# Product-key layer: batched second one-hot scaled on ScalarE, half the gate moves on VectorE, more products ahead of the run

## The chip, the cores and the metric

The kernel runs on one core of a Trainium2 chip, as one launch. The metric is the device time of an execution in microseconds. Five engines work side by side and each takes its own instructions in order: TensorE (PE; its weight loads are PEld), VectorE (DVE), ScalarE (ACT), GpSimd (POOL) and SyncE (SP), which here only issues transfers. They wait for one another by semaphores.

## The reference, cut to what matters

Two transformer blocks with mixtures of experts run first, then a block with a convolution and a recurrence. The change touches what stands at the very end, a product-key expert layer over 512 tokens of 1024 features. For each token and each of 8 heads it picks 16 of 128 x 128 experts and a gate for each; every expert is a row of `peer_u` and a row of `peer_v`.

```python
s1 = jnp.einsum('bshd,hnd->bshn', q[..., :half], peer_k1)
s2 = jnp.einsum('bshd,hnd->bshn', q[..., half:], peer_k2)
v1, i1 = lax.top_k(s1, PEER_TOPK)
v2, i2 = lax.top_k(s2, PEER_TOPK)
cand = (v1[..., :, None] + v2[..., None, :]).reshape(bsz, seq, PEER_HEADS, PEER_TOPK * PEER_TOPK)
sc, ci = lax.top_k(cand, PEER_TOPK)
experts = (jnp.take_along_axis(i1, ci // PEER_TOPK, axis=-1) * PEER_NKEYS
           + jnp.take_along_axis(i2, ci % PEER_TOPK, axis=-1))
gates = jax.nn.softmax(sc, axis=-1)
...
u_sel = jnp.take(peer_u, eb, axis=0)
z = jnp.einsum('td,tkd->tk', hb, u_sel)
act = jax.nn.gelu(z, approximate=False) * gb
return jnp.einsum('tk,tkd->td', act, jnp.take(peer_v, eb, axis=0))
```

## The kernel before

Tokens 384 to 511 (the last of four tiles) are done by rows: each of their 128 picks gathers a row of `peer_u` and a row of `peer_v` for 128 tokens at once (`row`, on GpSimd's queue), VectorE takes the dot product (`dot`) and adds the row times its gelu and gate (`add`). Tokens 0 to 383 are done densely: all 128 blocks of 128 experts are multiplied out, and a table `gd` of gates, zero where an expert was not picked, is multiplied onto the result.

A dense block a has two halves. `zed(a)` is the product of a block of `peer_ut` with the tokens: 8 steps of 3 matmuls (24 of 384 columns), then a gelu on ScalarE. The result stays in one of NZ = 17 tiles or, for the last ND blocks, goes to DRAM (`zd`) and comes back. The y half multiplies the result with the gates (`hid`, on GpSimd) and takes 18 matmuls of 512 columns with a block of `peer_v`. Each weight is split in two parts (`weight`): ScalarE rounds it to `whi`, and another engine subtracts to get `wlo`; the matmuls with `wlo` wait for that. Raw, high and low parts have four buffers each.

The layer runs in this order. `peer_pre` normalizes. `peer_pick` takes the picks (`peer_top`, then a loop over the tiles 3, 0, 1, 2 on VectorE, with transposes on TensorE). `peer_gates` builds `gd`: for each 8 tokens, VectorE makes one-hots (`hots`: 128 places against rows, and against columns times the gate), TensorE multiplies them token by token in two groups of four, the results move out of PSUM into `stage`, and each 16 tokens are stored. After the last store, the run goes over the 128 blocks: a product `zed(a + NZ)` and the y half of block a, until no products are left, then y halves alone; `turns` spreads the gathered rows over them, FAST of them while there are products.

Products of the first blocks and of the last ND come ahead of the run. They are a generator, `more`, and `ahead(n)` takes n of its steps; `peer_pick` calls it once a tile and `peer_gates` twice in 8 tokens, and what is left is done after the gates. The order on each engine is not that of the code: a scheduler places the instructions by its own estimate, and `issue_after` adds a few constraints. Line numbers are those of the profile of before.

Of the kernel before, what the change touches and what calls it, by code (L numbers as in the profile page):

```python
# [18 lines left out]
NEG = -1.0e30  # L19
# [6 lines left out]
class Net:  # L26
    def __init__(self, nc, tc, ctx, A, out, dbg=None):
# [3 lines left out]
        # what the weights' splits are queued behind: those of the next chunks, and of all others  # L31
# [18 lines left out]
    def consts(self):  # L50
# [5 lines left out]
        # NEG where key > query, for the block on the diagonal  # L56
# [8 lines left out]
        # before[s, t] = 1 where s < t  # L65
# [3 lines left out]
        # 16, 15, ... 1  # L69
# [6 lines left out]
        # token and, less 2 ** 20, its rows among the results of first and second choices  # L76
# [5 lines left out]
        # tri[s, t] = 1 where s <= t  # L82
# [6 lines left out]
    def wtile(self, tag, dt):  # L89
        """The stream's own buffers and, where a layer has room for them, more"""  # L90
        if self.over:
            return self.over.tile([128, 1024], dt, tag=tag + "o", bufs=1, name=tag)
        k = self.turn[tag] = self.turn.get(tag, 0) + 1
        n = self.extra.get(tag, 0) if self.more else 0
        if n and k % (n + 4) >= 4:
            return self.more.tile([128, 1024], dt, tag=tag + "x", bufs=n, name=tag)
        return self.wp.tile([128, 1024], dt, tag=tag, bufs=4, name=tag)

    def raw(self, src, key=None):
        """key: of a chunk that may have been loaded ahead"""  # L100
# [7 lines left out]
    def weight(self, src, w=1024, eng=None, key=None):  # L108
        """One chunk of up to [128, 1024] as the sum of two float32r tiles."""
# [11 lines left out]
    def mm3(self, out, l, r, start, stop):  # L121
        """out += (l0 + l1)^T (r0 + r1) without the product of the two low parts."""
# [8 lines left out]
    def rsqrt(self, x, n, name, bufs=2):  # L131
        """1 / sqrt(x) of an SBUF tile [p, n], by a first guess and three Newton steps."""
# [15 lines left out]
    def silu_row(self, src, pool):  # L148
        """silu of a row of features, on all partitions"""
# [6 lines left out]
    def ada(self, c, w, mod, cols, how="V", bufs=3, lag=2):  # L156
        """The six vectors as columns: column 8 v + k of mod has the features 128 k .. of vector v; how: by turns on
        VectorE (V) or on GpSimd and ScalarE (S). A generator that stops after each column, so that other work can run
        between; a column is done lag steps later. Its weights come into bufs tiles of the pool self.ring."""
# [34 lines left out]
    def bcast_cols(self, out, cols, n=4):  # L194
        """out[m, 128 i + t] = cols[t, i]"""
# [5 lines left out]
    def col_sum(self, x, n, pool, square, acc=None):  # L201
        """Sums over the features of x [128, n, tokens] (squared) as columns [128 tokens, tiles] in PSUM; acc: the sums
        over n"""
# [32 lines left out]
    def spread(self, t, sh, hi, lo, c):  # L236
        """hi + lo = t + sh, which, where c is odd, also goes to t"""
# [9 lines left out]
    def rms(self, x, pool, acc=None):  # L247
        """1 / sqrt(mean square + eps) of the tokens of x [128, 8, tokens], tokens on partitions"""
# [6 lines left out]
    def modulate(self, x, r, a, sh, h, pool, bufs=3):  # L255
        """h = x * r * a + sh: whole, or split in two"""
# [17 lines left out]
    def first_mod(self, x, gain, c, w, mod, hp, pool):  # L274
        """h = rmsnorm(x) * gain * (1 + sc) + sh, features on partitions, split in two, while sh and sc come in"""
# [29 lines left out]
    def head(self, prep, o, pt, pool):  # L305
        """One head in stages; prep gives score(i, ps, n), which fills ps[:, :n] with the logits of query block i, and
        the values; o: [64 rows, 512] f32"""
# [47 lines left out]
    def heads(self, quart, oT, pool, steps, early, first):  # L355
        """quart(q), a generator, prepares four heads and leaves their prep functions in the list it is given. The
        stages of a head run between those of its neighbours; first, a generator, between those of the first four, and
        steps of each quarter's heads the conditioning's. early: steps of the second four before the first head."""
        nc = self.nc
        ready, run = [], []  # L360
        # the weights of query block i and key block j, keys on partitions, at i + 3 j
# [33 lines left out]
    def fox_cum(self, h, cq, ck, room, keep):  # L395
        """Running sums of the log forget gates, as bfloat16 parts: head 4 j + m on rows 32 m .. of cell j"""
# [44 lines left out]
    def fox_heads(self, h, oT, keep, pool):  # L441
# [7 lines left out]
        def quart(quart, ready):  # L449
            qk = []  # L450
            for which, g in ((0, gq), (1, gk)):
# [14 lines left out]
                # the query's rows also carry the softmax scale 1/8  # L466
# [14 lines left out]
        def prep(quart, hh, qk, v):  # L481
            st = []
            for which in range(2):
                raw, r = qk[which]
                # twice, for the high and the low part
# [31 lines left out]
    def proj_tok(self, ps, h, ws, i):  # L517
        """ps[tok, n] = h[:, tokens of tile i]^T w for a weight of n columns in chunks of 1024 / n K tiles"""
# [9 lines left out]
    def split(self, src, pool, tag):  # L528
        """[128, n, 512] float32 as the sum of two float32r tiles"""
# [9 lines left out]
    def out_proj(self, x, oT, w, g1, pool, then=None):  # L539
        """x += g1 * (o w), features on partitions; then(c), when x's chunk c is done"""  # L540
# [15 lines left out]
    def rope_tables(self, keep, pool):  # L556
        """cos and sin of position * frequency, [128 tokens, 4, 16]"""
# [12 lines left out]
        for name, quarter in (("cos", 0.25), ("sin", 0.0)):  # L570
            # turns, rounded to whole ones, then angle - turns * 2 pi in three parts of 2 pi
# [16 lines left out]
    def rope(self, eng, x, cs, n, pool):  # L588
        """Turns x[128, 4, n, 32] in place"""
# [27 lines left out]
    def mla_begin(self, stack, x, gain, mod):  # L617
        """The latent rows are r (a x)^T w + sh^T w for h = a x r + sh, with r to come: opens the pool of a x and w, on the
        side that the layer before has left already, and gives a generator that loads w and works out sh^T w, and what is
        to be done when x's chunk c is there"""  # L620
# [25 lines left out]
    def mla(self, x, cs, room, pool):  # L646
# [3 lines left out]
        # the latent rows of the tokens, normed, features on partitions  # L650
# [1646 lines left out]
```

## Time and profile before

| | |
|---|---|
| median of three runs | 3077.49 us (3072.53 to 3083.78) |
| span of the profiled execution | 3077.5 us |
| TensorE busy over the span | 2764.6 us, 90% |
| VectorE busy | 2363.3 us, 77% |
| ScalarE busy | 1314.5 us, 43% |
| GpSimd busy | 1334.4 us, 43% |
| HBM read and written | 562.59 MB and 61.01 MB |

The profiled execution's span is as long as the median run, so nothing has to be added for what lies around it. The shares are means over stages that differ: the product-key layer takes the span from about 1700 us on. In it `peer_top` ends near 1842, the loop over the picks near 1941, the gates near 2157, and the run near 3045; the rest is the last normalization. Each stage is to be read by itself, by the busy time of every engine in that stretch.

### The profile page before, as it was taken

To read this page: it belongs to the slowest core of one execution; us is meant where nothing else is said; L and a number is where in the kernel's file an instruction comes from. 1 tells how busy PE (TensorE), PEld (TensorE's weight loads), DVE (VectorE), ACT (ScalarE), POOL (GpSimd) and SP (SyncE) were. 2 spreads that over 40 slices of the span, in tenths; PEclk is the share of its full clock that TensorE was granted. 3 is DMA by queue.
4 is the path that set the end of the run, shared out by engine and by line. 5 is a ranking of instruction groups with operands and counts; after the bars stand their busy time and mean duration, and the time that the engine had idled before them with its cause. 6 is when DMAs were issued, how large, how long until landed. Compare 5 with 4: busy or idle time off the path is not lost.

```text
span 3077.5 us, 42494 instructions
## 1 busy us (share of the span) xinstructions
PE 2764.6 (90%) x14989; PEld 2247.0 (73%) x14989; DVE 2363.3 (77%) x4756; ACT 1314.5 (43%) x2352; POOL 1334.4 (43%) x926
## 2 busy tenths in 40 slices
PE   2999978997889798899889897899999999999996
PEld 2877556686545566666766687889899999999885
DVE  7998458758975686688974799999677777777777
ACT  3344437734564573532432533334333333333332
POOL 3111027633211573006850345433566666666553
PEclk9999879998899899999988998999999999999998
DMA  6775159924535795220021223565999999999893
GB/s 220 239 242 182 65 193 314 342 96 139 185 124 188 236 331 205 90 72 19 1 78 37 88 85 122 201 227 185 322 312 321 313 318 325 326 314 315 285 328 112
DMA packets 230881, 622.81 MB, mean 202 GB/s; under 512 B 32796, under 2 KB 92492, under 8 KB 227192
## 3 DMA queue, kind: packets, MB, share of 16 engines
q1 hardware_dynamic: 130960, 429.82, 41.3%
q0 software_dynamic: 45120, 154.42, 14.7%
q10 hardware_dynamic: 54568, 35.66, 4.0%
q8 instruction: 122, 2.00, 0.3%
q14 instruction: 111, 0.91, 0.1%
HBM read 562.59 MB, written 61.01 MB: 203 GB/s over the span
## 4 chain that ended last, share of the span: by engine, by line
PE 39%; DVE 20%; DMA 4%; issue 2%; ACT 1%; POOL 1%; POOLq 0%; ACTq 0%; DVEq 0%; SPq 0%
PE y L126 5%; PE y L125 5%; PE acc L124 5%; PE acc L126 5%; PE acc L125 5%; PE y L124 5%; DVE a L1906 4%; DVE a L1902 2%; DMA wraw<-in_moe_w_dn_dram 2%; DMA wraw<-in_moe_w_gu_dram 2%; DVE s_y L1367 1%; DVE s_y L1526 1%; DVE wlo L118 1%; DVE wc L1550 1%; DVE t L1774 1%
## 5 line engine op out<-in xcount | busy, mean ns | idle before, releaser
L117 ACT ACTIVATE whi<-wraw 128x1024 fp32r<-128x1024 f32 (+1 forms) x552 | 576.5, 1049 | 458.2 <-PE acc L125 288.3
L118 DVE TENSOR_TENSOR wlo<-wraw,whi 128x1024 fp32r<-128x1024 f32 x410 | 565.5, 1390 | 265.6 <-ACT whi L117 264.4
L118 POOL TENSOR_TENSOR wlo<-wraw,whi 128x1024 fp32r<-128x1024 f32 (+1 forms) x142 | 367.1, 2592 | 478.9 <-ACT whi L117 445.2
L124 PE MATMUL acc<-h_hi,whi 128*128 128x384 f32 (+1 forms) x1328 | 478.0, 360 | 11.0 <-ACT z_out L1959 6.8
L126 PE MATMUL acc<-h_hi,wlo 128*128 128x384 f32 (+1 forms) x1328 | 472.5, 356 | 3.0 <-DVE wlo L118 3.0
L125 PE MATMUL acc<-h_lo,whi 128*128 128x384 f32 (+1 forms) x1328 | 473.1, 356 | 0.0
L126 PE MATMUL y<-whi,hid_l 128*128 128x512 f32 x768 | 302.3, 394 | 0.0
L1991 POOL DMA_INDIRECT gu<-in_peer_u_dram,e x128 | 206.5, 1613 | 219.0 <-DVE gu L2000 192.0
L125 PE MATMUL y<-wlo,hid_h 128*128 128x512 f32 x768 | 301.0, 392 | 0.0
L124 PE MATMUL y<-whi,hid_h 128*128 128x512 f32 x768 | 298.2, 388 | 0.0
L124 PEld LDWEIGHTS acc<-h_hi,whi 128*128 128x128 f32 x1328 | 255.1, 192 | 29.3 <-ACT z_out L1959 7.1
L126 PEld LDWEIGHTS acc<-h_hi,wlo 128*128 128x128 f32 x1328 | 254.4, 192 | 18.4 <-DVE wlo L118 4.0
L125 PEld LDWEIGHTS acc<-h_lo,whi 128*128 128x128 f32 x1328 | 255.1, 192 | 16.7 <-issue 1.0
L1991 POOL DMA_INDIRECT gv<-in_peer_v_dram,e x128 | 191.7, 1497 | 37.6 <-issue 27.6
L2056 ACT ACTIVATE hid_h<-hid 128x384 fp32r<-128x384 f32 x128 | 67.1, 524 | 289.2 <-PE y L125 252.7
L2032 DVE SCALAR_TENSOR_TENSOR y<-gv,pz,y 128x1024 f32<-128x1024 f32 x128 | 181.2, 1416 | 0.0
L182 DVE SCALAR_TENSOR_TENSOR ada_w<-ada_w,silu 128x1024 f32<-128x1024 f32 x138 | 174.0, 1261 | 8.7 <-DMA ada_w<-in_w_ada_dram 8.6
L125 PEld LDWEIGHTS y<-wlo,hid_h 128*128 128x128 f32 x768 | 144.2, 188 | 30.3 <-DVE wlo L118 0.3
L126 PEld LDWEIGHTS y<-whi,hid_l 128*128 128x128 f32 x768 | 144.3, 188 | 29.1
L124 PEld LDWEIGHTS y<-whi,hid_h 128*128 128x128 f32 x768 | 144.2, 188 | 28.8
L124 PE MATMUL acc<-whi,h_hi 128*128 128x256 f32 x480 | 140.6, 293 | 26.9 <-ACT whi L117 18.7
L2000 DVE SCALAR_TENSOR_TENSOR gu<-gu,hrow 128x1024 f32<-128x1024 f32 x128 | 163.2, 1275 | 0.0
(671 smaller groups left out, 6246.6 us busy)
## 6 DMA issues: line engine op xcount, KB each, us to landing
ada_w<-in_w_ada_dram SPq DMA_DIRECT2D x144, 512.0 KB, 4.2
wraw<-in_moe_w_gu_dram SPq DMA_DIRECT2D x128, 512.0 KB, 10.9
wraw<-in_peer_ut_dram SPq DMA_DIRECT2D x128, 512.0 KB, 6.3
wraw<-in_peer_v_dram SPq DMA_DIRECT2D x128, 512.0 KB, 5.9
wraw<-in_moe_w_dn_dram SPq DMA_DIRECT2D x64, 512.0 KB, 12.3
p_gd<-stage SPq DMA_DIRECT2D x24, 1024.0 KB, 3.9
gt<-p_gd ACTq DMA_DIRECT2D x16, 1536.0 KB, 22.0
wraw<-in_fox_w_in_dram SPq DMA_DIRECT2D x24, 512.0 KB, 4.7
```

The source lines that it names most:

```text
L117: nc.scalar.activation(hi[:, :w], r[:, :w], AF.Copy)
L118: self.low = eng.tensor_tensor(lo[:, :w], r[:, :w], hi[:, :w].bitcast(F32), op=OP.subtract).ins
L124: mm(out=out, lhsT=l[0], rhs=r[0], start=start, stop=False)
L125: mm(out=out, lhsT=l[0], rhs=r[1], start=False, stop=False)
L126: mm(out=out, lhsT=l[1], rhs=r[0], start=False, stop=stop)
L182: V.scalar_tensor_tensor(r, r, 1.0, c, op0=OP.mult, op1=OP.mult, accum_out=m)
L1902: V.tensor_tensor(a1, io[:, None, :].to_broadcast([128, 8, 128]), tr[:, 0, t0:t0 + 8, None].to_broadcast([128, 8, 128]), op=OP.is_equal)
L1906: V.tensor_scalar(a2[:, t, :], io, tr[:, 1, t0 + t:t0 + t + 1], tr[:, 2, t0 + t:t0 + t + 1], op0=OP.is_equal, op1=OP.mult)
L1991: nc.gpsimd.indirect_dma_start(out=u, out_offset=None, in_=src[:, :], in_offset=bass.IndirectOffsetOnAxis(ap=e3[:, k:k + 1], axis=0))
L2000: V.scalar_tensor_tensor(u, u, 1.0, hrow, op0=OP.mult, op1=OP.mult, accum_out=z8[b][:, k % 8:k % 8 + 1])
L2032: V.scalar_tensor_tensor(y3, vs.pop(k), z8[k // 8][:, k % 8:k % 8 + 1], y3, op0=OP.mult, op1=OP.add)
L2056: nc.scalar.activation(hh, hid, AF.Copy)
```

## The change

- `hots` makes both one-hots for 8 tokens at once on VectorE, and ScalarE scales the second one token by token with the gate. Before, the second one was eight instructions on VectorE, each comparing and multiplying.
- Of the two moves of gate products for 8 tokens, that of the second group goes to VectorE.
- ND goes from 29 to 41: 58 products come ahead of the run, before 46. `ahead` takes 64, 56, 28 and 28 steps in the four tiles of `peer_pick` (before 24 each), and 23 in 32 tokens of the gates (before 20).
- The first 14 of these products have their `wlo` from GpSimd, the other 44 from VectorE. Before, all came from GpSimd.
- 22 rows of `peer_u` are gathered and 20 dot products taken during the gates, one in 16 tokens (before 9 and 7, one in 32 tokens). FAST goes from 108 to 110, and the small tiles for the dot products have six buffers for three.

```diff
-        for i in (3, 0, 1, 2):
+        for i, n in ((3, 64), (0, 56), (1, 28), (2, 28)):
...
-            ahead(24)
+            ahead(n)
...
-            a1 = pool.tile([128, 8, 128], F32, tag="a1", bufs=3, name="a1")
-            V.tensor_tensor(a1, io[:, None, :].to_broadcast([128, 8, 128]),
-                            tr[:, 0, t0:t0 + 8, None].to_broadcast([128, 8, 128]), op=OP.is_equal)
-            a2 = pool.tile([128, 8, 128], F32, tag="a2", bufs=3, name="a2")
+            a = []
+            for j in range(2):
+                a.append(pool.tile([128, 8, 128], F32, tag=f"a{j}", bufs=3, name=f"a{j}"))
+                V.tensor_tensor(a[j], io[:, None, :].to_broadcast([128, 8, 128]),
+                                tr[:, j, t0:t0 + 8, None].to_broadcast([128, 8, 128]), op=OP.is_equal)
             for t in range(8):
-                V.tensor_scalar(a2[:, t, :], io, tr[:, 1, t0 + t:t0 + t + 1], tr[:, 2, t0 + t:t0 + t + 1],
-                                op0=OP.is_equal, op1=OP.mult)
-            return a1, a2
+                nc.scalar.activation(a[1][:, t, :], a[1][:, t, :], AF.Copy, scale=tr[:, 2, t0 + t:t0 + t + 1])
+            return a
...
-            if t0 % 32 == 8:
-                turn(t0 // 32)
+            if t0 % 16 == 8:
+                turn(t0 // 16)
...
-                ahead(2 + b)
+                ahead(2 + (b or t0 % 32 < 24))
                 k = t0 % 16 + b * 4
-                nc.scalar.activation(st[:, :, k:k + 4], pt.rearrange("p (t n) -> p n t", t=4), AF.Copy)
+                if b:
+                    V.tensor_copy(st[:, :, k:k + 4], pt.rearrange("p (t n) -> p n t", t=4))
+                else:
+                    nc.scalar.activation(st[:, :, k:k + 4], pt.rearrange("p (t n) -> p n t", t=4), AF.Copy)
...
-        NZ, ND, FAST = 17, 29, 108
+        NZ, ND, FAST, LEAD = 17, 41, 110, 20
...
-                load = lambda a, k: self.weight(A["peer_ut"][a], eng=nc.gpsimd)
+                load = lambda a, k: self.weight(A["peer_ut"][a], eng=nc.gpsimd if k < 14 else None)
...
-                    z8[b] = ahd.tile([128, 8], F32, tag="pz", bufs=3, name="pz")
+                    z8[b] = ahd.tile([128, 8], F32, tag="pz", bufs=6, name="pz")
...
-                if k < 7 + LD:
+                if k < LEAD + LD:
...
-                            if k + 7 + LD < 128:
-                                us[k + 7 + LD] = row(A["peer_u"], k + 7 + LD, ahd, "gu")
+                            if k + LEAD + LD < 128:
+                                us[k + LEAD + LD] = row(A["peer_u"], k + LEAD + LD, ahd, "gu")
...
-                            if k + 7 < 128:
-                                dot(k + 7)
+                            if k + LEAD < 128:
+                                dot(k + LEAD)
```

The order of the instructions moves with it. VectorE at the end of the picks, where the one-hots of the gates follow (`pge`, `ppr`, `pclf` are steps of a tile's picks, `a` is a one-hot), before:

```order
L1873 TENSOR_TENSOR pge<-pco,up_b 128x2048
L1876 TENSOR_TENSOR ppr<-pge,ptf 128x2048
L1878 TENSOR_REDUCE pclf<-ppr 128x128
L1902 TENSOR_TENSOR a_32245<-io,trip 128x1024
L1906 TENSOR_SCALAR a_32247<-io,trip 128x128 x8
```

And VectorE at the same place after the change:

```order
L1873 TENSOR_TENSOR pge<-pco,up_b 128x2048
L118 TENSOR_TENSOR wlo<-wraw,whi 128x1024
L1876 TENSOR_TENSOR ppr<-pge,ptf 128x2048
L118 TENSOR_TENSOR wlo<-wraw,whi 128x1024
L1878 TENSOR_REDUCE pclf<-ppr 128x128
L118 TENSOR_TENSOR wlo<-wraw,whi 128x1024 x3
L1904 TENSOR_TENSOR a_32585<-io,trip 128x1024
L1904 TENSOR_TENSOR a_32587<-io,trip 128x1024
```

Splits of weights now stand between the steps of the picks, eleven in all ahead of the first one-hot, and a one-hot of the columns is one instruction.

ScalarE at the start of the gates, before (`stage` is the target of the moves out of PSUM, `whi` a rounded weight, `z_out` a gelu on its way to DRAM):

```order
L1888 ACTIVATE trip<-tr 128x3x128
L117 ACTIVATE whi<-wraw 128x1024
L1959 ACTIVATE z_out<-acc 128x384
L1926 ACTIVATE stage<-S 128x128x4
L1926 ACTIVATE stage<-tr 128x128x4
```

And ScalarE there after:

```order
L1888 ACTIVATE trip<-tr 128x3x128
L1907 ACTIVATE a_32587<-a_32587,trip 128x128 x8
L1907 ACTIVATE a_32600<-a_32600,trip 128x128 x8
L1929 ACTIVATE stage<-S 128x128x4
L1962 ACTIVATE z_out<-acc 128x384
L1907 ACTIVATE a_32652<-a_32652,trip 128x128 x8
```

The scalings of the tokens ahead stand in front of the move of a group, and the moves of the second groups (`tr`) are gone from ScalarE.

TensorE where the run begins (`acc` is a product of `peer_ut`, `y` the sum over the blocks), before:

```order
L125 MATMUL acc<-h_lo,whi 128x384
L126 MATMUL acc<-h_hi,wlo 128x384
L124 MATMUL y_34549<-whi,hid_h 128x512
L125 MATMUL y_34549<-wlo,hid_h 128x512
L126 MATMUL y_34549<-whi,hid_l 128x512
```

And after, where the first y begins and where it ends:

```order
L124 MATMUL acc<-h_hi,whi 128x384
L125 MATMUL acc<-h_lo,whi 128x384
L124 MATMUL y_35050<-whi,hid_h 128x512
L125 MATMUL y_35050<-wlo,hid_h 128x512
```

```order
L125 MATMUL y_35055<-wlo,hid_h 128x512
L126 MATMUL y_35055<-whi,hid_l 128x512
L126 MATMUL acc<-h_hi,wlo 128x384
L124 MATMUL acc<-h_hi,whi 128x384
```

Before, the product that ends ahead of the first y is the last of those that come ahead of the run. Now the order has 71 product matmuls between the last gate group and the first y; 45 of them are the rest of the 58 products, and 26 belong to products of the run, the second of which is cut by the y.

## Rows read from the trace of the kernel before

**Rows 1.** Busy time by stretch: start:end, length, engines (instructions), granted clock, DMA share, GB/s.
```profile
1842.00:1941.00 99.00, 77.74 (x409) 76.36 (x408) 93.72 (x187) 29.03 (x40) 56.67 (x26) 0.88 0.39 119
1941.00:2157.00 216.00, 201.22 (x1366) 196.97 (x1365) 214.62 (x446) 91.32 (x147) 78.40 (x34) 0.98 0.60 212
...
2175.00:2225.00 50.00, 46.52 (x222) 40.95 (x221) 39.29 (x41) 18.18 (x27) 35.91 (x27) 0.97 1.00 350
2225.00:2850.00 625.00, 625.00 (x3169) 568.92 (x3168) 474.70 (x542) 222.41 (x315) 401.29 (x275) 1.00 0.92 318
...
2900.00:3045.00 145.00, 145.00 (x635) 118.77 (x634) 110.81 (x138) 51.73 (x72) 66.53 (x51) 1.00 0.80 271
```
**Rows 2.** Waits from 1842 to 2180: who waited for whom, total, times, longest.
```profile
PE tr L1887 <- DVE prf L1869: 10.3, 2, 9.1
...
PE acc L124 <- ACT z_out L1959: 6.8, 1, 6.8
```
**Rows 3.** TensorE in the gates, in order of time: start, length, instruction.
```profile
2108.79 1.05 PE L1922 MATMUL S<-a,a 128*128 128x128 f32 x8
...
2110.75 1.05 PE L1922 MATMUL tr<-a,a 128*128 128x128 f32 x8
...
2113.22 1.05 PE L1922 MATMUL S<-a,a 128*128 128x128 f32 x8
```
**Rows 4.** The handover to the run, four engines, in order of time.
```profile
2156.42 0.42 PE L124 MATMUL acc<-h_hi,whi 128*128 128x384 f32 x1
...
2156.70 0.60 ACT L1926 ACTIVATE stage<-tr 128x512 f32<-128x512 f32 x1 [1.36 <-PE tr L1922]
...
2172.76 1.04 POOL L2051 TENSOR_TENSOR hid<-x,gt 128x384 f32<-128x384 f32 x1 [9.97 <-issue]
...
2174.85 0.40 PE L124 MATMUL y<-whi,hid_h 128*128 128x512 f32 x1
```
**Rows 5.** TensorE from 2225 to 2850: busy us and matmuls of acc, then of y.
```profile
2225.00:2850.00 625.00, 326.32 (x1811) 1.00 0.92 318
...
2225.00:2850.00 625.00, 323.21 (x1358) 1.00 0.92 318
```
**Rows 6.** TensorE after its wait in the picks, in order of time; idle before in brackets.
```profile
1864.15 0.69 PE L124 MATMUL acc<-h_hi,whi 128*128 128x384 f32 x1 [6.77 <-ACT z_out L1959]
...
1867.20 0.52 PE L124 MATMUL acc<-h_hi,whi 128*128 128x384 f32 x1
1867.52 0.52 PE L125 MATMUL acc<-h_lo,whi 128*128 128x384 f32 x1
```
**Rows 7.** VectorE: one-hots without and beside a GpSimd split, splits, a dot product.
```profile
1940.86 1.23 DVE L1902 TENSOR_TENSOR a<-io,trip 128x1024 f32<-128x1024 f32 x1 [2.57 <-POOL io L1896]
1942.00 2.28 DVE L1906 TENSOR_SCALAR a<-io,trip 128x128 f32<-128x128 f32 x8
...
2151.41 4.21 DVE L1906 TENSOR_SCALAR a<-io,trip 128x128 f32<-128x128 f32 x8
2168.13 2.36 DVE L118 TENSOR_TENSOR wlo<-wraw,whi 128x1024 fp32r<-128x1024 f32 x2 [12.52 <-ACT whi L117]
...
2174.87 1.22 DVE L2000 SCALAR_TENSOR_TENSOR gu<-gu,hrow 128x1024 f32<-128x1024 f32 x1
```
**Rows 8.** Moves and scaled copies elsewhere: ns min/median/max by line, or start and length.
```profile
L961 DVE COPY h_row<-S x8: 661/684/692, 435.6 to 1006.2; 128x512 f32<-128x512 f32 x8
...
1506.04 1.08 ACT L1570 ACTIVATE dg<-id,wc_end 128x64 f32<-128x64 f32 x4
...
L327 ACT ACTIVATE P<-P,sm_r x32: 388/396/409, 129.8 to 920.3; 128x128 f32<-128x128 f32 x32
```
**Rows 9.** Two stretches of the run, as rows 1, and the issue of gt.
```profile
2475.00:2500.00 25.00, 25.00 (x128) 22.76 (x127) 19.09 (x23) 8.95 (x13) 15.70 (x12) 1.00 1.02 368
2725.00:2750.00 25.00, 25.00 (x129) 22.77 (x128) 19.08 (x23) 8.97 (x14) 16.92 (x12) 1.00 0.99 331
...
gt<-p_gd ACTq DMA_DIRECT2D x16, 1536.0 KB, 22.0
```

## Prediction

> **What bounds the kernel now.** The profiled execution's span is 3077.5 us, and the median of the three runs is 3077.49, so the sum is made against 3077.5 directly. I read the busy time by stretches first [rows 1], since the change touches only the last 1230 us. There are three stages there. From 1842 to 1941 (the picks) TensorE is busy 77.7 of 99 us and VectorE 93.7: VectorE sets the pace, and [rows 2] names what TensorE waited for: 10.3 us for the rows that VectorE works out for the transposes, 6.8 us for ScalarE's gelu. From 1941 to 2157 (the gates) VectorE is busy 214.6 of 216 us and TensorE 201.2. From 2225 on (the run over the 128 row blocks) TensorE is busy in every microsecond. So VectorE has no time left exactly where TensorE idles, and TensorE has none where everything else has some. Any product of `peer_ut` that TensorE can do earlier shortens the run by its full time; what it costs in the front depends on who is late there.
>
> **Prices of TensorE.** Where it never waits, a group of four gate products plus 6 product matmuls takes 1.96 us, with 9 it takes 2.47 [rows 3]. After the last gate group 105 product matmuls fill 2156.42 to 2174.85 [rows 4], 0.1755 us each; so a group is 1.96 - 6 x 0.1755 = 0.91, or 0.89 from the other row: 0.90. In 625 us of the run there are 1811 product and 1358 y matmuls [rows 5], 24 and 18 a block: 75.45 blocks, 8.28 us each. From 2900 to 3045 there are only y matmuls, 635 or 35.3 blocks: 4.11 us each [rows 1]. A product is worth 8.28 - 4.11 = 4.17 us in the run.
>
> **Products moved.** ND goes from 29 to 41, so 58 instead of 46 products come ahead and the run has 12 fewer: 12 x 4.17 = **-50.0 us**.
>
> **What they cost in the picks.** TensorE's order has 546 product matmuls ahead of the first gate product (415 before). The stall on ScalarE's gelu stays, since the exponential it queues behind is unmoved: TensorE has done 96 when it stops and goes on at 1864.15 [rows 6], the first 12 matmuls starting 0.32 us apart instead of 0.1755, which costs 1.7. The other 450 take 79.0: ready for the gates at 1944.9. VectorE now does 11 splits here at 1.18 us (two in 2.36 [rows 7]), +13.0. It ended the picks at 1938.3 (the first one-hot at 1940.86 after 2.57 us of waiting for GpSimd [rows 7]), and that wait goes, as GpSimd's queue no longer holds splits ahead of the iota. Six GpSimd splits that ran beside VectorE go too; eight one-hots take 4.21 us beside such a split and 2.28 without [rows 7], so each gives back about 1.9, together 11.6. VectorE is then ready at 1938.3 + 13.0 - 11.6 = 1939.7 and two batched one-hots and a scale later, near 1942.3, so TensorE's 1944.9 decides. If nothing is given back it is 1953.9, 9 us worse; that end stays in the range.
>
> **What they cost in the gates.** TensorE: 96 groups at 0.90 and 801 product matmuls (584 before) at 0.1755 are 86.4 + 140.6 = 227.0 us. VectorE: 96 batched one-hots at 1.14 (starts 1940.86 and 1942.00 [rows 7]) 109.4, 48 moves out of PSUM at 0.68 (a copy of that shape [rows 8]) 32.6, 33 splits at 1.18 38.9, 20 dot products at 1.22 [rows 7] 24.4: 205. The strided target of the move is not in the trace for VectorE; ScalarE writes it in 0.60 [rows 4], and a copy is not below that, so 0.60 to 0.68, and I take the latter. For 22 gathers beside VectorE I add nothing; at 1.93 each, as for a split, they would make 248. ScalarE: 91.3 us busy now [rows 1], less 48 moves at 0.60 (28.8), plus 384 scalings. Four scaled copies of 64 columns take 1.08, 0.27 each, and a single one of 128 columns 0.396 [rows 8]: 104 to 152; I take 0.28, since these stand back to back. Nine more products (801 - 584 over 24) at 1.39 us (the 33.7 us that are not moves, over 24.3 products) add 12.5. Together 179 to 227. So TensorE sets the pace with 227, from 1944.9 to 2171.9, against 2156.42 now: **+15.5 us**. The edge is small and the engines wait for one another in order: a VectorE move waits for the group's last product with splits behind it, on which later products wait. I add **+4.0**; the bounds are 0 and the 21 by which VectorE could exceed TensorE.
>
> [...]
>
> **The handover.** The last gate tile goes through a move, a store, the load of `gt` and a GpSimd product before the first y: 2156.42 to 2174.85, 18.4 us [rows 4]. Now 105 product matmuls cover that exactly. In the new order 71 stand there, 12.5 us, and TensorE waits 6 us, inside the +15.5 (the y still starts 18.4 after the last group). Of the 71, 26 belong to the run: 26 x 0.1755 = **-4.6**. [...]
>
> **The run.** A block of the first 70 (82 before) loads two weights of 0.524 MB, an eighth of `gt` (1.57 MB [rows 9]: 0.197) and 216 / 70 = 3.09 gathered rows of 0.524 (216 / 82 = 2.63 before): 2.86 MB instead of 2.63. At 8.28 us that is 346 GB/s against 318 now [rows 1]. There is a stretch with TensorE never idle at 368, and one whose engines were as full at 331 [rows 9]; at 368 nothing is lost, at 331 a block takes 8.65 and 70 lose 26. I take **+5**, nearer the first, as TensorE lost nothing in either. VectorE goes from 474.7 of 625 us (6.29 a block) to 6.29 + 0.254 x 2.44 = 6.9, with 110 / 70 - 108 / 82 = 0.254 more dot products and as many row sums a block, both at 1.22: hidden under 8.28. The 20 gathers done early are hidden in the gates, where 212 GB/s flow [rows 1].
>
> **Sum.** -50.0 + 15.5 + 4.0 - 4.6 + 1.8 + 5.0 = -28.3, so **3049**.
>
> **Rivals.** (1) All is hidden: no friction in gates, run or clock, -39.1, **3038**. For it: TensorE runs through stretches at 368 GB/s. [...] (2) VectorE becomes the bound of the front: gathers and in-order waits stretch its 205 to 248, 21 us over TensorE's 227 instead of my 4, **3066**. For it: it is the full engine now, and the change gives it 44 splits. Against: 336 one-hot instructions are gone from it, and so are most of the GpSimd splits that stretched it. (3) Slower: the transfers become the bound of the first 70 blocks. If the queues move no more than the 318 GB/s that they average now, a block takes 9.0 us and 70 lose 50, giving 3077.5 - 33.3 + 50 = **3094**. It decides from 8.28 + 33.3 / 70 = 8.76 us a block, 327 GB/s, on. For it: from 2175 to 2225 the engines were full at 350 and TensorE lost 3.5 us [rows 1]. Against: 368 beside a full TensorE. [...] That the change does not do what it says is excluded by the order, which shows the splits, scalings and products where the text puts them.
>
> **How the numbers follow.** The forecast (3043 to 3056) 0.45, rival 1 (3036 to 3043) 0.17, rival 2 (3056 to 3070) 0.20, transfers binding in part or whole (3070 to 3100) 0.13, none of these 0.05. Less than 0.3%, 9 us, can't be told from no change by a measurement of this kernel. Below 3068 lie forecast, rival 1 and most of rival 2: 0.80; within 9 us 0.11, from both late cases; above 3087, rival 3 in full: 0.09. Leaving out 2 in 10 gives 3036 to 3072.
>
> **What would show it.** Right: the first gate product near 1945, the first y near 2190, TensorE full in the gates and VectorE at about 0.9, a block of the run at 8.3 to 8.4 us and 346 GB/s, 58 blocks of y alone. Wrong: a first gate product after 1954 (VectorE in the picks), TensorE idle by 15 us or more in the gates, or blocks of 8.6 us and more with full DMA engines.

## The result, and the profile after

The changed kernel takes 3048.1 us (median of four runs, 3046.68 to 3050.83), the kernel before, beside it, 3080.64: 0.989 of it, with an interval of 0.986 to 0.991. The prediction was 3049. The profiled execution of after has a span of 3046.4 us (device time 3048.28). One run of e8 below took 3490.36 us at a granted clock of 0.74 and is left out of e8's ratio. Line numbers from 1904 on are up to three higher than before: the scalings are L1907, the moves L1927 (VectorE) and L1929 (ScalarE).

Busy time of after by stretch (columns as in [rows 1]), and of the fourth stretch the `acc` and the `y` matmuls alone:

```profile
1842.00:1946.00 104.00, 94.26 (x528) 92.94 (x528) 101.43 (x183) 38.01 (x52) 35.12 (x20) 0.97 0.51 149
1946.00:2175.00 229.00, 229.00 (x1583) 229.00 (x1582) 199.04 (x218) 189.05 (x502) 29.78 (x23) 1.00 0.74 259
2175.00:2225.00 50.00, 36.82 (x171) 32.63 (x170) 26.31 (x31) 11.54 (x18) 23.72 (x19) 0.86 0.83 286
2225.00:2780.00 555.00, 555.00 (x2815) 505.18 (x2814) 465.98 (x526) 198.55 (x283) 400.34 (x275) 1.00 0.97 350
2860.00:3010.00 150.00, 150.00 (x656) 122.89 (x655) 103.39 (x97) 52.86 (x72) 52.27 (x44) 1.00 0.72 229
...
2225.00:2780.00 555.00, 289.65 (x1609) 1.00 0.97 350
...
2225.00:2780.00 555.00, 286.99 (x1206) 1.00 0.97 350
```

Against [rows 1]: TensorE, busy 201.2 of 216 us in the gates before, is now busy all 229, and VectorE, full before, has 30 us left. In the run 1609 / 24 = 67.0 blocks take 555 us, 8.28 each, as before, at 350 instead of 318 GB/s; y alone takes 150 / (656 / 18) = 4.12. Only 2175 to 2225 got worse: TensorE is busy 36.8 of 50 us, before 46.5.

To say where the time went, I cut each profiled execution at five events on TensorE: its restart after the long wait for the gelu in the picks ([rows 6] before), the first and the last gate product, the first and the last y. The restart comes at 1864.15 before and at 1862.23 after, in code that the change doesn't touch; in the executions below it lies between 1856.8 and 1871.0. So I compare from there on (us):

| kernel | restart to first gate product | gates | to first y | first to last y | sum |
|---|---|---|---|---|---|
| before | 78.5 | 213.7 | 18.4 | 875.2 | 1185.8 |
| after | 85.4 | 226.8 | 22.1 | 822.5 | 1156.8 |
| after, once more (control) | 85.5 | 226.8 | 21.9 | 827.8 | 1162.0 |
| e1_hots | 78.0 | 196.2 | 19.8 | 877.2 | 1171.2 |
| e2_products | 90.2 | 239.4 | 18.0 | 826.6 | 1174.2 |
| e3_gpsimd_splits | 91.6 | 244.4 | 21.5 | 825.9 | 1183.4 |
| e11_splits_scalar | 91.9 | 243.6 | 17.6 | 824.5 | 1177.6 |
| e4_scalar_moves | 85.8 | 226.8 | 18.2 | 838.2 | 1169.0 |
| e5_late_rows | 85.2 | 226.9 | 21.3 | 824.0 | 1157.4 |
| e10_nd35 | 85.6 | 201.9 | 17.6 | 842.2 | 1147.3 |
| e6_cover21 | 85.3 | 214.1 | 21.8 | 828.6 | 1149.8 |
| e8_cover44 | 85.3 | 226.8 | 20.8 | 809.7 | 1142.6 |
| e9_nd44_21 | 85.7 | 214.1 | 34.9 | 820.8 | 1155.5 |
| e7_gt_parts | 85.6 | 226.8 | 18.9 | 837.1 | 1168.4 |

The column of the run also holds a difference that no edit makes. Two lines for y matmuls from 2300 to 2650 (ns: shortest, median, longest) and two stretches of y alone, each of after, then of e4:

```profile
L124 PE MATMUL y<-whi,hid_h x255: 388/388/391, 2300.1 to 2649.6; 128*128 128x512 f32 x128
2880.00:3000.00 120.00, 120.00 (x526) 1.00 0.75 237
...
L124 PE MATMUL y<-whi,hid_h x251: 396/397/398, 2301.3 to 2649.8; 128*128 128x512 f32 x126
2880.00:3000.00 120.00, 120.00 (x516) 1.00 0.79 254
```

The same matmuls take 388 or 397 ns in different executions, 526 or 516 of them fit in 120 us, and the granted clock reads 1.00 in both. e4, e7 and e9 were profiled at the longer time, with 515 or 516 in 120 us; all others have 525 or 526 there. That alone moves the run by up to 16 us, while the gates take 226.8 us in after, e4 and e7 alike. A smaller difference lies among the others: in e1, e2, e3, e6 and the control the product matmuls of the run start 174.7 to 176.7 ns apart, in before, after, e5, e8, e10 and e11 173.4; by their number (1654 in after) that is worth some 3 to 6 us. So the stages up to the first y are compared in the table, and whole kernels by their medians.

### The profile page after: what moved, and what is told of

Same layout as the page of the kernel before. It is cut to its first block, busy times and chain, and to the rows that moved or that the text cites. A ratio compares the mean times of both kernels' runs of the same rounds, so it can differ in the third digit from the quotient of the medians.

```text
span 3046.4 us, 42674 instructions
## 1 busy us (share of the span) xinstructions
PE 2748.0 (90%) x14989; PEld 2234.8 (73%) x14989; DVE 2342.8 (77%) x4500; ACT 1400.3 (46%) x2688; POOL 1235.6 (41%) x894
## 4 chain that ended last, share of the span: by engine, by line
PE 47%; DVE 13%; DMA 3%; issue 2%; ACT 1%; POOL 0%; POOLq 0%; DVEq 0%; ACTq 0%; SPq 0%
PE acc L124 7%; PE acc L125 7%; PE acc L126 7%; PE y L126 6%; PE y L125 6%; PE y L124 5%; DVE s_y L1367 1%; DMA wraw<-in_moe_w_gu_dram 1%; PE S L1922 1%; PE tr L1922 1%; DVE wlo L118 1%; DMA wraw<-in_moe_w_dn_dram 1%; DVE s_y L1526 1%; DVE wc L1550 1%; DVE t L1774 1%
## 5 line engine op out<-in xcount | busy, mean ns | idle before, releaser
L118 DVE TENSOR_TENSOR wlo<-wraw,whi 128x1024 fp32r<-128x1024 f32 x442 | 620.2, 1414 | 202.9 <-ACT whi L117 198.7
L118 POOL TENSOR_TENSOR wlo<-wraw,whi 128x1024 fp32r<-128x1024 f32 (+1 forms) x110 | 278.8, 2542 | 325.8 <-ACT whi L117 317.7
L1994 POOL DMA_INDIRECT gu<-in_peer_u_dram,e x128 | 196.0, 1531 | 243.2 <-DVE gu L2003 172.5
L1994 POOL DMA_INDIRECT gv<-in_peer_v_dram,e x128 | 200.1, 1563 | 155.1 <-DVE stage L1927 105.6
```

The costliest lines, as they stand in the source:

```text
L118: self.low = eng.tensor_tensor(lo[:, :w], r[:, :w], hi[:, :w].bitcast(F32), op=OP.subtract).ins
L1994: nc.gpsimd.indirect_dma_start(out=u, out_offset=None, in_=src[:, :], in_offset=bass.IndirectOffsetOnAxis(ap=e3[:, k:k + 1], axis=0))
```

## The experiments

All ratios are to the kernel before, whose median was 3080.05 us beside e1 to e4, 3085.57 beside e5 to e8 and 3082.01 beside e9 to e11 and the control. They are the recorded ratios; the quotients of the medians differ from them by up to 0.0014.

### Each half alone: e1_hots, e2_products

e1 is the kernel before with `hots` of the changed kernel, and nothing else:

```diff
-            for t in range(8):
-                V.tensor_scalar(a2[:, t, :], io, tr[:, 1, t0 + t:t0 + t + 1], tr[:, 2, t0 + t:t0 + t + 1],
-                                op0=OP.is_equal, op1=OP.mult)
+            for t in range(8):
+                nc.scalar.activation(a[1][:, t, :], a[1][:, t, :], AF.Copy, scale=tr[:, 2, t0 + t:t0 + t + 1])
```

> The kernel before with the one-hots alone: the second one batched by 8 tokens and scaled on ScalarE; products, splits, moves and rows as before. Theory (VectorE set the pace of the gates, and the batched one-hots free it): the gates then last as long as the next engine needs. TensorE has 96 groups at 0.90 and 577 products at 0.1755, 187.7 us; ScalarE has the 91.3 us of before and 384 scalings at 0.28, 199. So the gates shrink from 215.5 to about 200 us, the picks and the run stay, and the time falls by about 16 us (0.995 of before). Rival 1 (the whole gain is the one-hots', the products add nothing): 0.990, the time of the changed kernel. Rival 2 (the one-hots were stretched by the splits on GpSimd, and are so still): within 3 us of before.

Measured: 3067.78 us, 0.9957 (0.9942 to 0.9973). The gates of e1 and its longest wait there outside GpSimd:

```profile
1936.00:2131.00 195.00, 190.77 (x1336) 189.29 (x1335) 153.64 (x107) 189.51 (x523) 80.08 (x33) 1.00 0.66 225
...
DVE a L1904 <- PE tr L1922: 33.6, 21, 2.1
```

The gates shrink by 17.5 us, and VectorE now waits for TensorE (33.6 us, for a one-hot's buffer). So VectorE had set their pace, as the theory says, and neither rival fits: the whole gain is not here, nor is there none. TensorE and ScalarE, at 190.8 and 189.5 of 195, are level.

e2 is the kernel before with the products alone:

```diff
-            ahead(24)
+            ahead(n)
...
-                ahead(2 + b)
+                ahead(2 + (b or t0 % 32 < 24))
...
-        NZ, ND, FAST = 17, 29, 108
+        NZ, ND, FAST = 17, 41, 110
```

> The kernel before with the products alone: ND 41 and the counts of steps of the changed kernel, FAST 110; one-hots, moves, rows and the splits on GpSimd as before. Theory (VectorE has no time left in the front): 9 more splits on GpSimd beside VectorE in the gates at 1.9 us each make the gates 17 us longer (233), 6 more in the picks bring the first gate product to about 1950 (+10); the run is 50 us shorter, the handover loses 5 to 10 us as in the changed kernel: 13 to 18 us faster than before (0.995), 15 us slower than the changed kernel. Rival 1 (products fill idle time whoever splits): 0.990 or less, as the changed kernel. Rival 2 (splits on GpSimd come too late for the products, TensorE waits): no faster than before.

Measured: 3068.59 us, 0.9961 (0.9946 to 0.9975). The gates of e2, and VectorE's column one-hots in the gates of before and of e2 (busy us, mean ns):

```profile
1955.00:2192.00 237.00, 230.56 (x1561) 229.64 (x1562) 230.90 (x444) 101.69 (x161) 96.89 (x42) 0.99 0.64 218
...
L1906 DVE TENSOR_SCALAR a<-io,trip 128x128 f32<-128x128 f32 x375 | 149.4, 468 | 0.0
...
L1906 DVE TENSOR_SCALAR a<-io,trip 128x128 f32<-128x128 f32 x382 | 174.0, 524 | 0.0
```

The run is 48.6 us shorter, but picks and gates are 11.7 and 25.7 longer. VectorE has one split in the gates and nothing else more than before, yet a column one-hot takes 524 ns for 468, beside 33 splits on GpSimd for 25. The theory's direction holds, but the gates grew by 25.7 us where it had 17, and the gain is 11 us for its 13 to 18. Alone the halves save 12 and 11 us; the whole change, which also moves splits to VectorE, saves 29 to 33 (the control below, and the first measurement). The two halves do not add up to that by themselves, as e3 shows.

### Where the splits and the moves run: e3, e11, e4

e3 is the changed kernel with all splits of the early products on GpSimd; e11 has the moves on ScalarE as well:

```diff
-                load = lambda a, k: self.weight(A["peer_ut"][a], eng=nc.gpsimd if k < 14 else None)
+                load = lambda a, k: self.weight(A["peer_ut"][a], eng=nc.gpsimd)
```

> The changed kernel with all splits of the early products on GpSimd again. Theory (a split beside VectorE's one-hots costs VectorE about 1.9 us, more than the 1.2 us that it takes itself, but VectorE has 30 us to spare in the gates): gates stay at TensorE's 227 us and VectorE rises from 199 to about 220; in the picks 11 splits at 0.7 us more bring the first gate product from 1947.6 to about 1953: 0 to 8 us slower than the changed kernel. Rival (the move of splits to VectorE is what makes the products possible): VectorE becomes the bound or the products wait for late splits, TensorE idles 10 us or more in the gates, 15 us or more slower.

Measured: 3076.03 us, 0.999 (0.9974 to 1.0005). My theory falls, and the rival holds: the whole gain is gone. Stretches of the gates, of after and then of e3:

```profile
1970.00:2000.00 30.00, 30.00 (x208) 30.00 (x207) 29.41 (x34) 25.34 (x67) 4.53 (x4) 1.00 0.92 308
2060.00:2090.00 30.00, 30.00 (x209) 30.00 (x208) 26.52 (x28) 25.50 (x68) 0.42 (x1) 1.00 0.66 233
...
1970.00:2000.00 30.00, 27.29 (x180) 26.63 (x179) 30.00 (x27) 18.47 (x48) 22.59 (x11) 0.96 0.84 283
2000.00:2030.00 30.00, 25.77 (x166) 24.45 (x165) 30.00 (x33) 18.56 (x52) 18.82 (x11) 0.98 0.89 312
2030.00:2060.00 30.00, 26.12 (x169) 25.48 (x169) 30.00 (x26) 21.84 (x59) 15.39 (x8) 0.94 0.69 214
2060.00:2090.00 30.00, 30.00 (x207) 30.00 (x206) 24.65 (x20) 26.30 (x72) 12.03 (x6) 1.00 0.74 272
```

Over the gates VectorE is busy 199.8 of 241 us, not full; but from 1970 to 2060 it is busy in every microsecond, and there TensorE loses its time (all its stops in the gates lie between 1992 and 2043, but for one of 1.0 us at 1956). That is where the scheduler has put the rows and dot products of the gates: all 20 dot products of the gates lie between 1963 and 2043, not one in 16 tokens. In after VectorE is at 29.4 to 29.8 of 30 there too, with nothing to spare.

> The changed kernel with all splits of the early products on GpSimd (which alone was 28 us slower than the changed kernel) and also all moves out of PSUM on ScalarE. Theory (the loss came from VectorE's queue in order: one-hots and dot products stretched beside the splits, 200 us, and 38 us of waiting in front of its moves for TensorE's groups): without the moves VectorE has 168 us and no such wait, ScalarE 210, so the gates come back to 227 to 233 us from 244, and the time to within 10 us of the changed kernel. Rival (the products wait for splits that GpSimd delivers late): the gates stay at 240 us or more, and the time at 0.998 or more of before.

Measured: 3079.36 us, 0.9992 (0.9975 to 1.0009), gates 243.6 us: this theory falls as well. The rival's numbers came, but not for its reason: TensorE waits only 1.6 us in the gates for a split. Without moves VectorE is busy 165 of 241 us, and TensorE still stops. How its longest stop comes about, engine by engine (start, length, instruction, idle before):

```profile
2013.02 5.87 POOL L118 TENSOR_TENSOR wlo<-wraw,whi 128x1024 fp32r<-128x1024 f32 x2
2025.78 0.96 POOL L1991 DMA_INDIRECT gu<-in_peer_u_dram,e  x1 [0.15 <-issue]
...
2013.24 3.41 DVE L2000 SCALAR_TENSOR_TENSOR gu<-gu,hrow 128x1024 f32<-128x1024 f32 x1
2016.58 4.52 DVE L1904 TENSOR_TENSOR a<-io,trip 128x1024 f32<-128x1024 f32 x2
2022.17 1.21 DVE L2000 SCALAR_TENSOR_TENSOR gu<-gu,hrow 128x1024 f32<-128x1024 f32 x1
2027.71 2.49 DVE L2000 SCALAR_TENSOR_TENSOR gu<-gu,hrow 128x1024 f32<-128x1024 f32 x1 [4.32 <-DMA gu<-in_peer_u_dram,e]
2030.13 4.62 DVE L1904 TENSOR_TENSOR a<-io,trip 128x1024 f32<-128x1024 f32 x4
...
2032.52 1.28 ACT L1907 ACTIVATE a<-a,trip 128x128 f32<-128x128 f32 x4 [6.65 <-DVE a L1904]
...
2032.97 2.08 PE L1922 MATMUL S<-a,a 128*128 128x128 f32 x8 [5.70 <-ACT a L1907]
```

Two things come together. A dot product takes 1.21 us, but 3.41 when it starts with a split on GpSimd, and two one-hots take 4.52 for 2.35. Of the 20 dot products in the gates of e11, 16 took 1.21 or 1.22 us; the four that began beside a split took 3.51, 3.36, 3.41 and 2.49. Three of them stand beside a split with a row of its own (from 1995.12 for 2.40 us, 2006.30 for 2.51, 2026.75 for 2.36), and each ended 1.1 us after that split. What makes them wait the traces do not show. And the gathers stand between splits in GpSimd's queue: one at 2021.10, a split of 2.55 us from 2023.08, the next gather at 2025.78. A row comes late, VectorE waits 4.32 us for it with one-hots queued behind, ScalarE waits 6.65 for the one-hot, TensorE 5.70 for the scaled one.

So the gain needed the splits of the added products to leave GpSimd's queue, at least with the rows as early as here. e2 has all splits on GpSimd too, with the rows of before and without the new one-hots, and at 3068.59 us it is faster than e3. Whether the stretching or the late rows weigh more is open: splits on GpSimd with the one-hots of the change and the rows spread out wasn't tried.

e4 has the moves alone back on ScalarE:

```diff
-                if b:
-                    V.tensor_copy(st[:, :, k:k + 4], pt.rearrange("p (t n) -> p n t", t=4))
-                else:
-                    nc.scalar.activation(st[:, :, k:k + 4], pt.rearrange("p (t n) -> p n t", t=4), AF.Copy)
+                nc.scalar.activation(st[:, :, k:k + 4], pt.rearrange("p (t n) -> p n t", t=4), AF.Copy)
```

> The changed kernel with all moves out of PSUM on ScalarE again. ScalarE then has the 189 us that it has now in the 229 us of the gates, and 48 moves at 0.60, 218; VectorE 199 less 48 at 0.69, 166. Theory (TensorE sets the pace of the gates): within 3 us of the changed kernel, TensorE idle under 5 us in the gates. Rival (ScalarE, which works in order, is the bound at 218, and the groups wait for their moves): TensorE idle 10 us or more in the gates, 10 to 20 us slower.

Measured: 3052.97 us, 0.9904 (0.9887 to 0.9922); the gates take 226.8 us, TensorE idle for none of it, ScalarE at 204 of 225. The theory holds: in the gates this part of the change moves nothing. The gates of e4:

```profile
1951.00:2176.00 225.00, 225.00 (x1556) 225.00 (x1555) 168.65 (x168) 203.99 (x540) 38.93 (x23) 1.00 0.72 260
```

### Rows early or late: e5

```diff
-        NZ, ND, FAST, LEAD = 17, 41, 110, 20
+        NZ, ND, FAST, LEAD = 17, 41, 108, 7
...
-            if t0 % 16 == 8:
-                turn(t0 // 16)
+            if t0 % 32 == 8:
+                turn(t0 // 32)
```

> The changed kernel with the gathered rows as before: 9 rows and 7 dot products during the gates, one in 32 tokens, FAST 108. Theory (13 dot products at 1.22 us and 13 gathers lie beside a full TensorE wherever they stand; a block of the run has 3.09 rows either way): within 3 us of the changed kernel; VectorE in the gates 16 us less than its 199. Rival (the rows done early relieve the transfers of the run): a block of the first 70 takes over 8.4 us, 8 us or more slower.

Measured: 3050.17 us, 0.9896 (0.9878 to 0.9914); every stage is within 1.5 us of after's, VectorE busy 182.5 of 225 us in the gates. The theory holds. Its gates:

```profile
1944.00:2169.00 225.00, 225.00 (x1557) 225.00 (x1556) 182.48 (x187) 185.22 (x492) 11.10 (x10) 1.00 0.65 229
```

### What a product is worth: e10

```diff
-        NZ, ND, FAST, LEAD = 17, 41, 110, 20
+        NZ, ND, FAST, LEAD = 17, 35, 110, 20
...
-                ahead(2 + (b or t0 % 32 < 24))
+                ahead(2 + (b and t0 % 32 < 24))
```

> The changed kernel with half of the twelve products put back: ND 35, and 19 for 23 steps in 32 tokens of the gates, so that the handover has as many products as now (68). Theory (a product is worth 24 x 0.1755 = 4.21 us of TensorE ahead of the run and 4.17 in it, so one that fills no idle time gains nothing, and in the changed kernel the gates have none left): the gates shrink by 141 matmuls, 25 us, to 202, the run grows by 6 x 4.17 = 25: within 3 us of the changed kernel. Rival (each product moved ahead is a gain of its own): up to 25 us slower, 0.997 of before. If VectorE, with 192 us of work in 202, already holds up the gates, 5 to 10 us slower.

Beside it the changed kernel once more, as a control:

> The changed kernel once more, on the same chip as the three beside it, so that they can be compared with it and not only with before. Every theory expects 0.987 to 0.991 of before, about 3048 us.

Measured: 3048.25 us, 0.9892 (0.9863 to 0.9922), the control 3052.74, 0.9905 (0.9879 to 0.9931). The gates shrink by 24.9 us, the run grows by 19.7, and the kernel is no slower: the last six of the twelve products bring nothing. The gates of e10:

```profile
1951.00:2154.00 203.00, 203.00 (x1436) 203.00 (x1435) 191.00 (x212) 178.08 (x488) 28.52 (x23) 1.00 0.78 270
```

TensorE is full in them with six products fewer. The run of e10 has 144 product matmuls more than that of after, 25.0 us at 173.4 ns; it grows by less mainly because after's second stop of 4.16 us, described next, is not in it. So once TensorE is full in the gates, a product costs there what it saves in the run.

### The handover: e6, e8, e9, e7

In after the last gate tile takes 22.1 us to the first y. Its links, in order of time (PE's first product after the last group; VectorE's move; a weight load and the store on the sync engine's queue; the load of `gt`; GpSimd's product; the first y and a second stop):

```profile
2174.41 0.42 PE L124 MATMUL acc<-h_hi,whi 128*128 128x384 f32 x1
...
2175.46 0.68 DVE L1927 COPY stage<-tr 128x512 f32<-128x512 f32 x1
...
2175.57 0.33 SPq L105 DMA_DIRECT2D wraw<-in_peer_v_dram  x1
2176.17 0.33 SPq L1974 DMA_DIRECT2D p_gd<-stage  x1
...
2182.25 0.38 ACTq L2046 DMA_DIRECT2D gt<-p_gd  x1
...
2194.89 0.99 POOL L2054 TENSOR_TENSOR hid<-x,gt 128x384 f32<-128x384 f32 x1 [27.88 <-DMA gt<-p_gd]
...
2196.49 0.80 PE L124 MATMUL y<-whi,hid_h 128*128 128x512 f32 x1 [8.05 <-ACT hid_h L2059]
...
2209.66 0.73 PE L126 MATMUL y<-whi,hid_l 128*128 128x512 f32 x2 [4.16 <-DVE hid_l L2060]
```

The store and the issue of `gt` of before, for comparison (its last weight load ahead of the store on that queue is at 2154.79):

```profile
2157.33 0.33 SPq L1971 DMA_DIRECT2D p_gd<-stage  x1
...
2161.35 0.38 ACTq L2043 DMA_DIRECT2D gt<-p_gd  x1
```

With [rows 4]: from the product to the store's issue 1.76 us (0.91 before), to the load of `gt` 6.08 (4.02), to `hid` 12.64 (11.41), to the y 1.60 (2.09), 22.1 for 18.4. TensorE runs out of products and waits 8.05 us, works at a granted clock of 0.54 from 2196 to 2201 (y matmuls start 0.43 us apart, from 2200.8 on, at 1.00, 0.23), and stops again for 4.16, with the same pitch of 0.43 at a granted clock of 0.50 from 2211.0 to 2214.0.

In after the store stands 0.60 us behind a weight load of 512 KB on the same queue. So it does in the control, e3, e5 and e6, and their handovers take 21.3 to 22.1 us. Where the store goes ahead of that load (e2, e4, e11) or at least 1.8 us behind it (before, e10), it takes 17.6 to 18.4; e1, 1.6 us behind, has 19.8. But the place of the store does not settle it. In e8 and e9 it stands 0.60 us behind as well, their products outlast the chain, and `hid` starts 17.4 and 18.4 us after the last gate product, against 20.5 in after. The first `hid` of e8, whose last gate product is at 2183.11:

```profile
2200.49 1.03 POOL L2054 TENSOR_TENSOR hid<-x,gt 128x384 f32<-128x384 f32 x1 [24.76 <-DMA gt<-p_gd]
```

The load of `gt`, from its issue to `hid`, takes 9.5 us there, 9.8 in e4, 8.7 in e10 and 12.6 in after. Why it differs stays open; the order of the queue alone was not tried. Nor are the 3.7 us all lost to the move on VectorE: in e2, e4 and e11, whose last move is on ScalarE, the first y comes 3.9 to 4.5 us sooner than in after, but the second stop is 6.6 to 6.7 us instead of 4.16.

e6 keeps more of the same products for after the gates, e8 adds three products there, e9 does both:

```diff
-                ahead(2 + (b or t0 % 32 < 24))
+                ahead(2 + (b or t0 % 32 < 8))
```

```diff
-        NZ, ND, FAST, LEAD = 17, 41, 110, 20
+        NZ, ND, FAST, LEAD = 17, 44, 110, 20
```

> The changed kernel with 21 for 23 steps of products in 32 tokens of the gates: the same products ahead of the run, but 117 instead of 71 product matmuls between the last gate group and the first y. Theory (the handover is a chain of transfers of 18 to 22 us that 71 matmuls, 12.5 us, don't cover): the gates end 12.6 us sooner, 117 matmuls are 20.5 us, the 8.05 us of waiting before the first y and the half clock after it (2 to 4 us) go: 8 to 12 us faster than the changed kernel, 0.985 to 0.987 of before. Rival (the weights of more products take the queue from the store and the load of gt, and the chain grows by what the cover gains): within 3 us of the changed kernel.

> The changed kernel with ND 44 and the same counts of steps in picks and gates: three more products ahead of the run, all of them in the handover, so 117 instead of 71 product matmuls there. Theory: three products leave the run (3 x 4.17 = 12.5 us), 26 matmuls of the run no longer stand in the handover (4.6), so 8 us faster, and 2 to 4 us of half clock more: 8 to 12 us faster than the changed kernel, 0.985 to 0.987 of before. Rival 1 (three products cost in the handover what they save in the run): within 3 us. Rival 2 (67 instead of 70 blocks carry the same rows and the transfers bind): a block of the run takes over 8.4 us, slower than the changed kernel.

> The changed kernel with both ways of covering the handover at once: ND 44, and 21 for 23 steps in 32 tokens of the gates: 189 product matmuls, 33 us, before the first y, more than the chain of 18 to 22 us. Theory (only idle time can be gained, and 117 matmuls cover the chain already): as the kernel with ND 44 alone, 5 to 14 us faster than the changed kernel, 0.983 to 0.988 of before. Rival (more cover gains more): a further 12 us, 0.980 or less.

Measured: e6 3040.88 us, 0.9867 (0.9846 to 0.9888), in the range expected; e8 3044.57, 0.9881 (0.9856 to 0.9905), above its 0.985 to 0.987, though its interval holds them; e9 3039.4, 0.9849 (0.9822 to 0.9875). The first y of e6 and of e8:

```profile
2177.96 0.50 PE L124 MATMUL y<-whi,hid_h 128*128 128x512 f32 x1 [0.78 <-ACT hid_h L2059]
...
2203.90 0.39 PE L124 MATMUL y<-whi,hid_h 128*128 128x512 f32 x1
```

The wait of 8.05 us becomes 0.78 and nothing, and the chain did not grow with the added weights (the first y comes after 21.8 and 20.8 us, in e8 when its products end). As whole kernels e6 and e8 are not apart from the changed one by their intervals; e9 is apart from the control beside it, 13 us faster, though not from the first measurement of the changed kernel (0.986 to 0.991). Its interval also holds e6's ratio and nearly meets e8's, so more cover than the chain needs shows no further gain.

e7 loads the first `gt` in two parts, so that only 2 of 24 groups wait for the last store:

```diff
+                        for b0, b1 in ((0, 22), (22, 24)) if a == 0 else ((0, 24),):
+                            nc.scalar.dma_start(out=gt[0][:, b0:b1].rearrange("p b n t -> p b (n t)"),
+                                                in_=gd[b0:b1, :, a:a + 8, :].rearrange("b p n t -> p b (n t)"))
```

> The changed kernel with the first load of gt in two parts, 22 and 2 of the 24 groups of 16 tokens, so that only the small one waits for the last store. Theory (the load of 12.6 us after the last store is the longest link of the handover): the first part is issued when ScalarE comes to it, about 2180, and takes about 11 us, the second stands behind a gelu near 2183; the first y comes 3 to 5 us sooner, 3 to 5 us faster than the changed kernel. Rival (the transfers share the engines, so two parts take as long as one): within 2 us.

Measured: 3052.01 us, 0.9891 (0.987 to 0.9911), no change. The first y comes 18.9 us after the last gate group, 3.2 sooner, but then (VectorE, and TensorE's first matmul with `hid_l`):

```profile
2196.50 1.26 DVE L2003 SCALAR_TENSOR_TENSOR gu<-gu,hrow 128x1024 f32<-128x1024 f32 x1 [9.11 <-DMA gu<-in_peer_u_dram,e]
2199.26 1.02 DVE L2061 TENSOR_TENSOR hid_l<-hid,hid_h 128x384 fp32r<-128x384 f32 x2
...
2199.87 1.65 PE L126 MATMUL y<-whi,hid_l 128*128 128x512 f32 x3 [7.47 <-DVE hid_l L2061]
```

VectorE waits 9.11 us for a gathered row with `hid_l` queued behind, and TensorE stops for 7.47 us: the wait moved. Neither the theory nor the rival had this.

## Why the prediction was right, point by point

By the cuts of the table, the sum of the prediction (-28.3) and what came (-29.0):

| step | predicted | measured |
|---|---|---|
| picks, restart to first gate product | +2.2 | +6.9 |
| gates, with friction | +17.3 | +13.1 |
| last gate product to first y | 0 | +3.7 |
| run: products, credit, clock, transfers | -47.8 | -52.7 |

- **Products, -50.** Right: 8.28 and 4.12 us a block against 8.28 and 4.11. Only the credit of 4.6 and the +1.8 for the clock after the wait come with them, so -52.8 without the transfers; -52.7 was measured. The second stop of 4.16 us is in that, against 3.5 us of stops in the run of before; the prediction had neither.
- **Clock after the wait, +1.8.** No run shows this term of the sum. In its place after shows ten y matmuls, at a granted clock of 0.54, that take 4.28 us, from 2196.49 to 2200.77, where ten at a pitch of 0.23 take 2.3: 2.0 us more; and seven from 2211.01 to 2213.99, at 0.50, 1.4 us more by the same count.
- **Transfers, +5.** Not needed: 350 GB/s with TensorE full, no loss, and rival 3 (318 GB/s, 3094) fell. So the 318 of before was what the kernel asked for, not the most that the queues move; in after 381 GB/s ran from 2200 to 2225.
- **Picks.** The 79.0 us of products and TensorE as the one that decides were right. I missed 3.3 us of new waits between 1908 and 1919, 2.2 of them for a split that VectorE now does in its order, 1.0 for gelus. Under 2 us are left over.
- **Gates.** The 227.0 us of TensorE's terms measured 226.8; the friction of 4 was 0. VectorE was busy 199 (205 predicted), a move took 0.69 us (0.68), ScalarE 189 (in 179 to 227). A scaling took 116.4 / 377 = 0.31 us, between my 0.28 and the 0.396 of the single copies; that is busy time divided by the count, as neighbours overlap, and the mean length of one is 0.392 us. The 384 small scalings did not make ScalarE the bound: in e4, with 48 moves more, it is busy 204 of 225 us and TensorE idles for none of them.
- **Margin on VectorE.** My 0.9 was a mean over the gates. Its share was 0.99 from 1970 to 2060 and 0.88 in the 30 us after, and lower still behind them, since the dot products lie at the front (the 20 of the gates between 1961 and 2072); rival 2 was nearer than the mean says, and e3, with splits and gathers on GpSimd, shows something like it come true.
- **Handover.** This is the step that failed: I took its 18.4 us as fixed and got 22.1, and TensorE waited 8.05 us and then 4.16 instead of 6. The links that grew are those up to the store (0.9 us), from it to the load of `gt` (2.1) and that load (1.2), less 0.5 in the last. Of the engines there I had read TensorE, VectorE and ScalarE and not the sync engine's queue, where a weight load now stands just ahead of the store; that this is the cause is not shown.

So the total was right in part because errors cancelled: 8.4 us too little for picks and handover, 9 too much for friction and transfers. The medians moved by 32.5 us; the 3.5 beyond the cuts' 29.0 are within the spread of the restart.

The largest gap was in the reason, not the sum. I priced twelve products at 4.17 us each and then took off what they cost. e10 says the same shorter: only the time in which TensorE idled could be gained, some six products fill it, and the rest are moved for nothing. In before TensorE idled 14.5 us in the picks behind the restart and 14.8 us in the gates, 29.3 together, which is the size of the gain.

## What to carry to other kernels

Moving work of a full engine ahead of its stage gains only what it fills of that engine's idle time; sum the idle time first (here 29.3 us), and stop when it is gone. A mean busy share hides where a scheduler has packed the work (VectorE in the gates of e3: 199.8 of 241 us, but 90 of 90 from 1970 to 2060), so read the margin of an engine in short stretches before leaning on it. Cover the last chain of transfers between two stages with products that are kept for it: here that took away the wait before the first y (8.05 us to 0.78 and none), where the last six products had brought nothing.

## What the runs showed that I had not expected

TensorE's pace in the run differs by 2% between executions (388 or 397 ns for the same y matmul, 526 or 516 in 120 us) at a granted clock that reads 1.00, and the restart in the picks by 14 us in code that is the same. Neither follows an edit, and their cause stays open. Together they are larger than most differences measured here.
